# Seven-product gates in a two-layer encoder: a second tile for the raw weight sums, branch c run to its end first, wider gaps between the differences' transfers

## The chip, the cores and the metric

The kernel runs on one core of one Trainium2 chip. The metric is device time in microseconds (us) of one execution. Before the change it is 1827.98 us, the median of three runs (1826.03 to 1829.21).

## The reference

Two layers of an encoder over 512 positions with 1024 channels. In each layer three token mixers (differential attention, a convolution module, neighbourhood attention) give ya, yb and yc with 512 channels each. Each is projected to 1024 channels and multiplied by a sigmoid gate that is itself a projection of the normalised input.

```
h = rmsnorm(x, norm_mix[i])
proj = h @ w_in[i]
...
ga, gb, gc = jnp.split(jax.nn.sigmoid(gates), 3, axis=-1)
merged = (ga * (ya @ w_br_a[i]) + gb * (yb @ w_br_b[i])
          + gc * (yc @ w_br_c[i]))
x = x + merged @ w_o[i]
```

A SwiGLU feed-forward network and a gated embedding follow in each layer, and one norm at the end.

## The kernel before, in words

Channels lie on the 128 partitions and the 512 positions along the free axis, so a tensor of 1024 channels is eight tiles of 128x512. Everything is float32, and a matrix product runs as three matmuls for each block (`mm3`, L178): both operands are split into a high and a low part of a reduced float32 form, and high x high, high x low and low x high are summed. The high part is made by a copy on ScalarE (ACT, L144), the low part by a subtraction on VectorE (DVE, L158). So each weight is loaded by SyncE's DMA queue (SP), split by ACT and then by DVE, and used by TensorE (PE).

The order of the work in one layer, around the change: the gates of branch c (`gate_c`), the first two of branch b (`gate_b` m = 0, 1), the products of branch c (`branch_c`, one per m, with `w_br_c`), two more gates of branch b (m = 2, 3), then `merge_a`, then the convolution's norm, the rest of gate b, and the merge.

`merge_a` makes the gates of branch a by pairs of output tiles with a seven-product scheme (`gates`, L847): a 2x2 block product is done with seven products instead of eight. Its weights are a11, a12 and a22, as they are, and four sums of blocks, s1 to s4. The sums are built in a tile called the raw sums (`raw`, 128x1024). SP loads two blocks into it (L864, L865), GpSimd's queue (POOL) adds two more by accumulating DMAs (L869), ACT and DVE split the result into s1 and s2, then DVE turns the same tile in place into s3 and s4 (L161, L158), and these are split too. There is one such tile, named `gatec_v` in the profile, for all four pairs of a layer: the loads of a pair can start only when the splits of the pair before have read it. The other operands of the products are differences of the input (`t1` to `t4`), which `scaled` adds up on POOL into a DRAM buffer `tq` during an earlier stage (L265), and `differences` loads and splits by quarters during branch c.

PE does for each pair, in this order: a11 | s1, s3, a12 | s2, a22, s4. At the strokes (the `yield`s) `merge_a` puts in the products of a branch as a filling (`branch_pair`): for pair 0 those of branch c with m = 6 and 7, which `branch_c` leaves out, for the others those of branch a of the pair before. A holds s3's sum on top of a copy of C (a11's product), Q is a copy of A, and the copies are made by ACT (L144). The product with s4 is written into A as well, and must wait until ACT has copied A away. In the profile, PE's rows are `mergea_mm` for C, A and Q, `mergea_tr` or `branchc_tr` for T (the product of s1), `branchc_sc` for the filling of pair 0; `mergea_b` and `mergea_rp` are the splits of s4 and s3; `mergea_wh` and `mergea_wl` are the splits of weights and of s1 and s2.

A fourth strand is the aside chain (`aside`): 16 taps of the convolution for one block of channels. Each tap is an ACT instruction into one tile (`conv_rb`), which POOL then adds to the sum by an accumulating DMA (L593, `conv_z<-conv_rb`); the next tap can start only when that DMA has read the tile. Its steps are placed in ACT's queue behind certain instructions of the other stages (`beside`).

PE's order is that of the program. The queues of the other engines are ordered by the framework's scheduler by priority; weight loads and their splits are drawn ahead (`high_priority`). Every engine works through its queue in order, so an instruction that waits holds all behind it.

Of the kernel before, what the change touches and what calls it, by code (L numbers as in the profile page):

```python
# [15 lines left out]
ALU = mybir.AluOpType  # L16
# [4 lines left out]
P = 128  # L21
# [5 lines left out]
KD = 8  # L27
# [35 lines left out]
class Net:  # L63
# [181 lines left out]
    def scaled(self, xs):  # L245

        c = self.i * PAR_L
        self.nc.vector.tensor_scalar(self.neg[:, self.i * KD:self.i * KD + KD],
                                     self.parts[:, c:c + KD], -1.0, None, ALU.mult)
        for k, x in enumerate(xs):  # L250
            yield 1
            self.tt(x, x, self.rb, ALU.mult)
            self.hs.append(self.operand(x, self.par(self.i, "mix", k), "h"))
            f, n = self.sb("t", [P, 2, 256]), self.i * KD + k
            for half in range(2):
                g = self.par(self.i, "mix", k) if half == k % 2 else self.neg[:, n:n + 1]
                self.act(f[:, half], x[:, half * 256:half * 256 + 256], AF.Copy, scale=g)
            self.nc.gpsimd.dma_start(self.fd[:, k % 2 * 2:k % 2 * 2 + 2, k // 2], f)
        t1, t2, t3, t4 = (self.tq[:, n] for n in range(4))
        b11, b12, b21, b22 = (self.fd[:, n] for n in range(4))  # L260
        for out, src, add in ((t1, b11, 0), (t3, b22, 0), (t1, b12, 1), (t3, b12, 1), (t2, t1, 0),
                              (t2, b22, 1), (t4, t2, 0), (t4, b21, 1)):
            yield 4
            kw = dict(accum_op=ALU.add) if add else {}
            self.nc.gpsimd.dma_start(out, src, **kw)  # L265

# [186 lines left out]
    def layer(self, i, h, xsrc, xs):  # L453
        self.i, self.h = i, h
        zs, cs = [], []
        self.todo, self.other = self.taps(zs, cs), self.aside(zs)
        self.glu(zs)
        if i == 0:
            self.lambdas()
        yc, ya, yb = [], [], []  # L460
        sn, sd = {}, {}
        self.natten_in(0, sn, yc)
        self.drain(self.renorm)
        self.h = self.hs
        self.natten_v(sn)
        last = self.glu_last(zs)
        self.natten_in(1, sn, yc)
        next(last)
        self.natten_in(2, sn, yc)
        next(last)  # L470
        self.natten_in(3, sn, yc)
        acc, gb = [], []
        self.diff_in(0, sd, ya)
        self.diff_v(0, sd)
        self.diff_in(1, sd, ya)
        self.gate_c(acc, 0)
        self.diff_in(2, sd, ya)
        self.diff_v(1, sd)
        self.diff_in(3, sd, ya)
        for m in range(1, KD):  # L480
            self.gate_c(acc, m)
        self.bs, self.raw = [], self.sb("v", [P, 1024])
        for m in range(2):
            self.gate_b(gb, m, AF.Copy, None)
        for g in acc + gb:
            self.act(g, g, AF.Sigmoid, table="sigmoid")
        self.branch_c(acc, yc)
        for m in range(2, 4):
            self.gate_b(gb, m, AF.Sigmoid, "sigmoid")
        self.merge_a(yc, ya, acc)  # L490
        conv = self.run(self.conv(cs, yb))
        pairs = self.inputs()
        for m in range(4, KD):
            self.gate_b(gb, m, AF.Sigmoid, "sigmoid")
            for n in ((0, 1), (2,), (3,), ())[m - 4]:
                self.input_block(pairs, n)
        self.drain(conv)
        mg = self.merge_b(yb, acc, gb)
        ws = self.pair_weights(4)
        x, h = self.w_o(mg, xsrc)  # L500
        self.input_pair(ws, pairs, 4)
        h = self.ffn(h, x)
        return self.ple(h, x, xs, self.inputs())
# [305 lines left out]
    def branch_c(self, acc, ys):  # L809
        self.phase = "branchc"  # L810
        quarters = self.differences()
        for m in range(KD - 2):
            ps = self.ps("mm")
            self.gemm(ps, self.a["w_br_c"][self.i, m], ys)
            self.background(self.tt(acc[m], acc[m], ps, ALU.mult), self.bg["branchc"])
            next(quarters, None)
            if m % 3 == 2:
                next(quarters, None)
        for _ in quarters:
            pass  # L820

# [25 lines left out]
    def gates(self, m, out):  # L847

        self.phase = "mergea"
        nc, raw = self.nc, self.raw  # L850
        wg, wu = (self.a["w_ga"][self.i, m + u] for u in range(2))
        ws = {}
        lo, up = slice(0, 512), slice(512, 1024)

        def halve(hi, lo, src, names):
            self.split(hi, lo, src)
            for q, name in enumerate(names):
                c = slice(q * 512, q * 512 + 512)
                ws[name] = (hi[:, c], lo[:, c])

        wide = lambda: (self.sb("wh", [P, 1024], F32R), self.sb("wl", [P, 1024], F32R))
        with self.tc.high_priority(offset=min(self.w_ahead, self.tc.cur_priority - self.p0)):
            g, a22 = self.sb("wr", [P, 1024]), self.sb("r", [P, 512])
            nc.sync.dma_start(raw[:, lo], wg[:, lo])  # L864
            nc.sync.dma_start(raw[:, up], wu[:, up])  # L865
            nc.sync.dma_start(g, wg)
            nc.sync.dma_start(a22, wu[:, up])
            for q in (lo, up):
                nc.gpsimd.dma_start(raw[:, q], wu[:, lo], accum_op=ALU.add)  # L869
            halve(*wide(), g, ("a11", "a12"))  # L870
            halve(self.sb("kh", [P, 512], F32R), self.sb("a", [P, 512], F32R), a22, ("a22",))
            halve(*wide(), raw, ("s1", "s2"))
            self.stt(raw[:, lo], raw[:, lo], -1.0, a22, ALU.mult, ALU.subtract)
            self.tt(raw[:, up], g[:, up], raw[:, lo], ALU.subtract)
            for name, q, tag in (("s3", lo, "rp"), ("s4", up, "b")):
                halve(*(self.sb(tag, [P, 512], F32R) for _ in range(2)), raw[:, q], (name,))
        C, A, Q = (self.ps("mm", (P, 256)) for _ in range(3))

        def product(ps, w, b, first=False):
            wh, wl = ws[w]  # L880
            for k in range(4):
                c, both = slice(k * P, k * P + P), self.bs[k][b]
                self.mm3(ps, wh[:, c], wl[:, c], both[:, 0], both[:, 1], first and k == 0, k == 3,
                         skip_group_check=True)
                if k % 2:
                    self.chunk()

        gg, uu = self.sb("t", [P, 2, 256]), self.sb("t", [P, 2, 256])
        product(C, "a11", "b11", True)
        self.act(A, C, AF.Copy)  # L890
        yield
        T = self.ps("tr", (P, 256))
        product(T, "s1", "t3", True)
        self.act(uu[:, 0], T, AF.Copy)
        product(A, "s3", "t2")
        self.background(self.act(Q, A, AF.Copy), self.bg["mergea"])
        product(C, "a12", "b21")
        self.act(gg[:, 0], C, AF.Sigmoid, table="sigmoid")
        yield
        product(A, "s2", "t1")  # L900
        self.act(uu[:, 1], A, AF.Copy)
        product(Q, "a22", "t4")
        self.tt(uu[:, 1], uu[:, 1], uu[:, 0], ALU.add)
        last = self.tt(uu[:, 0], Q, uu[:, 0], ALU.add)
        product(A, "s4", "b22")
        self.act(gg[:, 1], A, AF.Sigmoid, table="sigmoid")
        self.beside(self.act(uu, uu, AF.Sigmoid, table="sigmoid", scale=-1.0))
        self.background(last, self.bg["mergea2"])
        out += [g.rearrange("p a b -> p (a b)") for g in (gg, uu)]
        yield  # L910
# [19 lines left out]
            take(acc[m + u], pb, m + u)  # L930
            yield

    def merge_a(self, yc, ys, acc):
        gs = []

        def times(a, pb, m):
            last = self.tt(a, a, pb, ALU.mult)
            self.background(last, self.bg["branchc"])

        def gated(a, pb, m):  # L940
            g = gs[m]
# [2 lines left out]

        for n in range(5):
            pair = self.gates(2 * n, gs) if n < 4 else iter(())
            if n:
                fill = self.branch_pair("w_br_a", ys, acc, 2 * n - 2, gated)
            else:
                fill = self.branch_pair("w_br_c", yc, acc, 6, times)  # L950
            for g in (pair, fill, fill, pair, fill, pair):
                next(g, None)

# [750 lines left out]
```

## Time and profile before

| | |
|---|---|
| median of three runs | 1827.98 us (1826.03 to 1829.21) |
| the profiled execution | 1828.74 us, of it the span 1827.0 us |
| mean granted TensorE clock | 0.983 |
| chain that ended last | PE 26% of the span, DVE 1%, all others 0% as the page rounds them |
| DMA | 289.02 MB, mean 158 GB/s |

Times in the rows are microseconds from the start of the span. A row of the timeline gives the start, the length, the engine, the line and the tiles (output first), and in brackets how long the engine had been idle before and whom it had waited for. The length of a PE row is that of one matmul from start to end; since they overlap, the time of a product is read from the starts. Layer 0's stage of the change lies at about 320 to 420 us, layer 1's at about 1224 to 1320 us.

### The profile page before, as it was taken

The numbers are of one execution on the slowest core, as the hardware profiler recorded it, in microseconds if no ns is written. First come the engines' busy times: TensorE is split into PE (matmuls) and PEld (weight loads), VectorE is DVE, ScalarE is ACT, GpSimd is POOL, SyncE is SP. The second block draws the span as 40 slices with busy tenths as digits, with TensorE's granted clock in tenths as the row PEclk, the third lists the DMA queues.
The fourth block names the chain that finished last, engine by engine and source line by source line (L and its number), as shares of the span: only waits on it lengthen the run. The fifth ranks groups of instructions, "written<-read, shape, count | busy, mean of one in ns | idle before, by whom it ended". The sixth has DMA issues, their size and how long they took to land. (4 is left out here: it accounts for less than half of the span.)

```text
span 1827.0 us, 26061 instructions
## 1 busy us (share of the span) xinstructions
PE 1769.6 (97%) x9258; PEld 1518.3 (83%) x9258; DVE 1427.7 (78%) x2366; ACT 1030.3 (56%) x1867; POOL 182.4 (10%) x208
## 2 busy tenths in 40 slices
PE   9999999887999999999999999998899999999998
PEld 7789888786888888888888888887778888888887
DVE  7877987756889778697787788787577996877876
ACT  5576556344577456474555655564445773655744
POOL 0100001121111011000010000011201210101000
PEclk9999999898999999999999999998899999999999
DMA  6885644574757556453459755356738573655432
GB/s 225 246 220 156 166 115 135 151 157 109 213 157 195 140 154 159 135 141 110 150 187 244 209 146 162 99 153 141 165 101 242 150 199 114 171 152 152 111 101 93
DMA packets 133954, 289.02 MB, mean 158 GB/s; under 512 B 18880, under 2 KB 29888, under 8 KB 133824
## 3 DMA queue, kind: packets, MB, share of 16 engines
q1 hardware_dynamic: 107920, 234.13, 41.7%
q0 software_dynamic: 25184, 51.92, 15.8%
q8 instruction: 73, 1.20, 0.3%
q10 hardware_dynamic: 720, 1.31, 0.2%
q14 instruction: 57, 0.47, 0.1%
HBM read 234.33 MB, written 19.92 MB: 139 GB/s over the span
## 5 line engine op out<-in xcount | busy, mean ns | idle before, releaser
L161 DVE SCALAR_TENSOR_TENSOR conv_z<-glu_z,pre_par,conv_z 128x512 f32<-128x512 f32 x210 | 157.0, 747 | 4.5 <-DMA conv_z<-conv_rb 1.6
L144 ACT ACTIVATE ffn_wh<-ffn_wr 128x1024 fp32r<-128x1024 f32 (+1 forms) x92 | 92.7, 1021 | 99.4 <-PE ffn_mm L181 66.4
L1160 POOL DMA_DIRECT2D ffn_qk<-w_fu x88 | 78.3, 972 | 589.6 <-DMA ffn_qk<-w_fu 277.9
L158 DVE TENSOR_TENSOR ffn_wl<-ffn_wr,ffn_wh 128x1024 fp32r<-128x1024 f32 (+1 forms) x92 | 107.1, 1175 | 21.0 <-ACT ffn_wh L144 20.5
L158 DVE TENSOR_TENSOR ffn_t<-ffn_mm,wo_rb 128x512 f32<-128x512 f32 (+1 forms) x46 | 31.1, 677 | 51.6 <-PE ffn_mm L182 51.6
L158 DVE TENSOR_TENSOR ffn_wl<-ffn_qk,ffn_wh 128x1024 fp32r<-128x1024 f32 x44 | 53.6, 1218 | 11.0 <-ACT ffn_wh L144 10.9
L144 ACT ACTIVATE ffn_wh<-ffn_qk 128x1024 fp32r<-128x1024 f32 x44 | 46.7, 1061 | 26.8 <-PE ffn_mm L181 16.2
L144 ACT ACTIVATE diff_a<-diff_sc,diff_s 128x512 f32<-128x512 f32 x32 | 22.1, 689 | 66.9 <-DVE diff_s L1074 66.6
L180 PE MATMUL ffn_mm<-ffn_v,ffn_wh 128*128 128x512 f32 x132 | 51.4, 389 | 0.0
L181 PE MATMUL ffn_mm<-ffn_v,ffn_wh 128*128 128x512 f32 x132 | 51.4, 389 | 0.0
L182 PE MATMUL ffn_mm<-ffn_v,ffn_wl 128*128 128x512 f32 x132 | 51.3, 389 | 0.0
L180 PE MATMUL ffn_mm<-ffn_y,ffn_wh 128*128 128x512 f32 x132 | 51.3, 389 | 0.0
L181 PE MATMUL ffn_mm<-ffn_y,ffn_wh 128*128 128x512 f32 x132 | 51.3, 389 | 0.0
L182 PE MATMUL ffn_mm<-ffn_y,ffn_wl 128*128 128x512 f32 x132 | 51.3, 389 | 0.0
L144 ACT ACTIVATE natten_wh<-natten_wr 128x1024 fp32r<-128x1024 f32 x24 | 25.3, 1056 | 40.4 <-PE natten_sc L734 21.5
L1194 PE MATMUL ffn_sc<-wo_h,ffn_wh 128*128 128x512 f32 x176 | 48.0, 394 | 0.0
L158 DVE TENSOR_TENSOR ffn_t<-ffn_t,ffn_e 128x256 f32<-128x256 f32 x84 | 46.2, 550 | 1.0 <-ACT ffn_e L144 0.9
L593 POOL DMA_DIRECT2D conv_z<-conv_rb x30 | 27.0, 899 | 180.5 <-ACT conv_rb L144 128.7
L1074 DVE TENSOR_REDUCE diff_s<-diff_sc 128x1 f32<-128x512 f32 x64 | 42.1, 682 | 2.2 <-PE diff_sc L981 2.2
L1194 PE MATMUL ffn_mm<-wo_h,ffn_wh 128*128 128x512 f32 x160 | 43.6, 394 | 0.0
L226 POOL TENSOR_TENSOR diff_rc<-diff_sm,pre_power 128x4 f32<-128x4 f32 x8 | 8.9, 1113 | 347.5 <-DVE diff_sm L161 347.5
L144 ACT ACTIVATE natten_b<-natten_b,natten_s 128x256 f32<-128x256 f32 x64 | 30.5, 500 | 21.1 <-DVE natten_s L767 21.0
(1038 smaller groups left out, 6393.5 us busy)
## 6 DMA issues: line engine op xcount, KB each, us to landing
ffn_qk<-w_fu POOLq DMA_DIRECT2D x88, 256.0 KB, 6.6
ffn_wr<-w_fg SPq DMA_DIRECT2D x44, 512.0 KB, 4.2
ffn_wr<-w_fd SPq DMA_DIRECT2D x32, 448.0 KB, 3.9
ffn_r<-w_fu SPq DMA_DIRECT2D x44, 256.0 KB, 2.8
ffn_qk<-w_fg SPq DMA_DIRECT2D x44, 256.0 KB, 3.3
ffn_qk<-w_fu SPq DMA_DIRECT2D x44, 256.0 KB, 3.5
natten_wr<-w_in SPq DMA_DIRECT2D x16, 512.0 KB, 5.3
diff_wr<-w_in SPq DMA_DIRECT2D x16, 512.0 KB, 4.5
```

The costliest lines, as they stand in the source:

```text
L144: i = self.nc.scalar.activation(out, in_, func, **kw)
L158: return self.nc.vector.tensor_tensor(out, a, b, op)
L161: return self.nc.vector.scalar_tensor_tensor(out, a, s, b, op0, op1)
L180: mm(out, wh, ah, start=first, stop=False, **kw)
L181: mm(out, wh, al, start=False, stop=False, **kw)
L182: mm(out, wl, ah, start=False, stop=last, **kw)
L226: nc.gpsimd.tensor_tensor(col, ms, self.power, ALU.pow)
L593: self.nc.gpsimd.dma_start(c, t, accum_op=ALU.add)
L1074: nc.vector.tensor_reduce(out=m[:, u:u + 1], in_=sc, op=ALU.max, axis=AX.X, negate=True)
L1160: nc.gpsimd.dma_start(q, wu[:, lo], accum_op=ALU.add)
L1194: mm(out, wh[:, c], bs[k][b], start=first and k == 0, stop=False, skip_group_check=True)
```

## The change

There are three edits.

1. In `scaled` eight units of other work instead of four stand between the transfers that add up `tq` (`yield 8`).
2. `branch_c` makes all eight products itself; the filling of pair 0 in `merge_a` is empty. The quarters of `differences` advance by one per product (before, by two after the third and the sixth).
3. A second tile holds raw sums (`gateb_y` in the names below); pairs 0 and 2 use the first, pairs 1 and 3 the second.

```diff
@@ scaled
-            yield 4
+            yield 8
             kw = dict(accum_op=ALU.add) if add else {}
             self.nc.gpsimd.dma_start(out, src, **kw)
@@ layer
-        self.bs, self.raw = [], self.sb("v", [P, 1024])
+        self.bs, self.raws = [], [self.sb("v", [P, 1024])]
...
-        self.merge_a(yc, ya, acc)
+        self.merge_a(ya, acc)
@@ branch_c
-        for m in range(KD - 2):
+        for m in range(KD):
...
             next(quarters, None)
-            if m % 3 == 2:
-                next(quarters, None)
@@ gates
-        nc, raw = self.nc, self.raw
+        nc, raw = self.nc, self.raws[m // 2 % 2]
@@ merge_a
-    def merge_a(self, yc, ys, acc):
+    def merge_a(self, ys, acc):
         gs = []
-
-        def times(a, pb, m):
-            last = self.tt(a, a, pb, ALU.mult)
-            self.background(last, self.bg["branchc"])
+        self.raws.append(self.sb("y", [P, 1024]))
...
-            if n:
-                fill = self.branch_pair("w_br_a", ys, acc, 2 * n - 2, gated)
-            else:
-                fill = self.branch_pair("w_br_c", yc, acc, 6, times)
+            fill = self.branch_pair("w_br_a", ys, acc, 2 * n - 2, gated) if n else iter(())
```

On TensorE, at pair 0 in layer 0: the end of a11 (mergea_mm) and what follows it, before the change.

```order
L180 MATMUL mergea_mm<-glu_h,mergea_wh 128x256
L181 MATMUL mergea_mm<-glu_h,mergea_wh 128x256
L182 MATMUL mergea_mm<-glu_h,mergea_wl 128x256
L180 MATMUL branchc_sc<-natten_y,branchc_wh 128x512
L181 MATMUL branchc_sc<-natten_y,branchc_wh 128x512
L182 MATMUL branchc_sc<-natten_y,branchc_wl 128x512
```

The same place after the change.

```order
L180 MATMUL mergea_mm<-glu_h,mergea_wh 128x256
L181 MATMUL mergea_mm<-glu_h,mergea_wh 128x256
L182 MATMUL mergea_mm<-glu_h,mergea_wl 128x256
L180 MATMUL mergea_tr<-branchc_qk,mergea_wh 128x256
L181 MATMUL mergea_tr<-branchc_qk,mergea_wh 128x256
L182 MATMUL mergea_tr<-branchc_qk,mergea_wl 128x256
```

Before, twelve matmuls of branch c stood between a11 and s1's product, and twelve more behind a12; now s1's product follows a11 at once, and those 24 stand ahead of gate b's m = 2.

On POOL's queue from the fourth norm of the heads (diff_rc) to the adds of the first gates (gatec_x), layer 0, before the change; gatec_v<-w_ga are the accumulations of raw sums, conv_z<-conv_rb those of the aside taps.

```order
L226 TENSOR_TENSOR diff_rc<-diff_sm,pre_power 128x4
L593 DMA conv_z<-conv_rb 128x512
L869 DMA gatec_v<-w_ga 128x512 x2
L593 DMA conv_z<-conv_rb 128x512
L869 DMA gatec_v<-w_ga 128x512 x2
L593 DMA conv_z<-conv_rb 128x512
L869 DMA gatec_v<-w_ga 128x512 x2
L943 DMA gatec_x<-mergea_t 128x512
L943 DMA gatec_x<-mergea_t 128x512
L869 DMA gatec_v<-w_ga 128x512
L593 DMA conv_z<-conv_rb 128x512
L869 DMA gatec_v<-w_ga 128x512
```

The same place after the change.

```order
L226 TENSOR_TENSOR diff_rc<-diff_sm,pre_power 128x4
L867 DMA gateb_y<-w_ga 128x512 x2
L593 DMA conv_z<-conv_rb 128x512
L867 DMA gatec_v<-w_ga 128x512 x2
L593 DMA conv_z<-conv_rb 128x512
L867 DMA gatec_v<-w_ga 128x512 x2
L867 DMA gateb_y<-w_ga 128x512
L593 DMA conv_z<-conv_rb 128x512
L938 DMA gatec_x<-mergea_t 128x512
L867 DMA gateb_y<-w_ga 128x512
L938 DMA gatec_x<-mergea_t 128x512
L593 DMA conv_z<-conv_rb 128x512
```

Pair 1's sums (gateb_y) now come first, pair 0's behind them and behind a tap; pair 2's (the second gatec_v) have moved ahead by one pair.

On SP's queue, from the loads of a11 and a12 (mergea_wr<-w_ga) on, before the change; mergea_wr<-w_br_a and branchc_wr are the weights of the fillings.

```order
L866 DMA mergea_wr<-w_ga 128x1024
L830 DMA branchc_t<-tq 128x2x256
L830 DMA branchc_t<-tq 128x2x256
L830 DMA branchc_t<-tq 128x2x256
L920 DMA branchc_wr<-w_br_c 128x512 x2
L866 DMA mergea_wr<-w_ga 128x1024
L864 DMA gatec_v<-w_ga 128x512
L865 DMA gatec_v<-w_ga 128x512
L920 DMA mergea_wr<-w_br_a 128x512 x2
```

The same place after the change.

```order
L864 DMA mergea_wr<-w_ga 128x1024
L864 DMA mergea_wr<-w_ga 128x1024
L862 DMA gateb_y<-w_ga 128x512
L863 DMA gateb_y<-w_ga 128x512
L918 DMA mergea_wr<-w_br_a 128x512 x2
L862 DMA gatec_v<-w_ga 128x512
L863 DMA gatec_v<-w_ga 128x512
L865 DMA mergea_r<-w_ga 128x512
L864 DMA mergea_wr<-w_ga 128x1024
```

The raw loads of pair 1 and the weights of branch a's first filling now stand ahead of the raw loads of pair 0. POOL's eight transfers into tq stand in the same order, with the same waits, before and after.

## The prediction

> **What bounds the kernel now.** The page's first rows come first: they say which engine is the bound.
>
> ```profile
> PE 1769.6 (97%) x9258; PEld 1518.3 (83%) x9258; DVE 1427.7 (78%) x2366; ACT 1030.3 (56%) x1867; POOL 182.4 (10%) x208
> ```
>
> TensorE (PE) works 97% of the span. A change that keeps its matmuls, as this one does, can win only PE's waits and what a lowered clock adds. So the next view is PE's waits, summed by instruction and releaser (us in total, times, longest).
>
> ```profile
> PE mergea_mm L180 <- ACT mergea_t L144: 26.5, 8, 5.4
> PE branchc_sc L180 <- ACT branchc_wh L144: 8.8, 2, 4.5
> PE conv_tr L629 <- ACT conv_rp L144: 8.8, 2, 4.4
> PE diff_tr L230 <- POOL diff_rc L226: 1.9, 2, 1.4
> ```
>
> The first two rows are in the stage that the change touches. Eight times, four pairs in two layers, the product with s4 waits for ACT's copy of A; twice the first product of the branch c fill waits for its weights. PE's timeline gives the places, with the idle time before each in brackets.
>
> ```profile
> 320.45 0.39 PE L180 MATMUL gateb_mm<-glu_h,gateb_wh 128*128 128x512 f32 x1
> 331.33 0.28 PE L180 MATMUL mergea_mm<-glu_h,mergea_wh 128*128 128x256 f32 x1
> 332.65 0.28 PE L182 MATMUL mergea_mm<-glu_h,mergea_wl 128*128 128x256 f32 x1
> 337.26 0.67 PE L180 MATMUL branchc_sc<-natten_y,branchc_wh 128*128 128x512 f32 x1 [4.33 <-ACT branchc_wh L144]
> 355.52 0.58 PE L180 MATMUL mergea_mm<-glu_h,mergea_b 128*128 128x256 f32 x1 [3.33 <-ACT mergea_t L144]
> 374.69 0.39 PE L180 MATMUL mergea_mm<-glu_h,mergea_b 128*128 128x256 f32 x1 [0.78 <-ACT mergea_t L144]
> 395.21 0.39 PE L180 MATMUL mergea_mm<-glu_h,mergea_b 128*128 128x256 f32 x1 [4.73 <-ACT mergea_t L144]
> 417.96 0.58 PE L180 MATMUL mergea_mm<-glu_h,mergea_b 128*128 128x256 f32 x1 [5.44 <-ACT mergea_t L144]
> ...
> 1240.64 0.80 PE L180 MATMUL branchc_sc<-natten_y,branchc_wh 128*128 128x512 f32 x1 [4.48 <-ACT branchc_wh L144]
> 1258.41 0.39 PE L180 MATMUL mergea_mm<-ple_h,mergea_b 128*128 128x256 f32 x1 [2.28 <-ACT mergea_t L144]
> 1276.80 0.39 PE L180 MATMUL mergea_mm<-ple_h,mergea_b 128*128 128x256 f32 x1 [1.08 <-ACT mergea_t L144]
> 1296.31 0.39 PE L180 MATMUL mergea_mm<-ple_h,mergea_b 128*128 128x256 f32 x1 [3.73 <-ACT mergea_t L144]
> 1318.75 0.58 PE L180 MATMUL mergea_mm<-ple_h,mergea_b 128*128 128x256 f32 x1 [5.13 <-ACT mergea_t L144]
> ```
>
> Between 320.45 and 331.33 stand the 48 matmuls of gate b's m=2, 3: 0.227 us a step. The twelve of a11 (331.33 to 332.65) step by 0.12. From one s4 product to the next PE has 84 steps of 0.12 and 24 of 0.227, 15.5 us; the spacings are 19.17, 20.52 and 22.75 in layer 0 and 18.39, 19.51 and 22.44 in layer 1. A stall costs more than itself, as three windows show (length, PE's busy time and matmuls, granted clock, DMA share, GB/s).
>
> ```profile
> 354.00:362.00 8.00, 6.48 (x29) 0.57 0.52 176
> 395.00:400.00 5.00, 4.79 (x26) 0.66 0.93 202
> 1276.00:1280.00 4.00, 3.21 (x26) 1.00 0.45 101
> ```
>
> After the stall of 3.33 the clock averages 0.57 over 8 us; after 1.08 it stays 1.00. Layer 0's 19.17 is 15.5 of work, 0.78 of stall and 2.9 of slow clock; layer 1's 18.39 holds 1.8 of it. On this the Trainium skill, "TensorE: Matmul & The Clock Gate", Part 1, speaks: the clock halves after about 3.4 us idle. By that, neither pair 0's 3.33 nor its 2.28 would slow it, the gain of 2.8 and 2.0 worked out below would fall away, and the time would be 1822.2. The trace says otherwise (0.57 after 3.33), and it decides.
>
> **Who holds the stalls.** ACT's and POOL's rows for the raw sums (gatec_v is their tile):
>
> ```profile
> 327.71 0.92 POOL L593 DMA_DIRECT2D conv_z<-conv_rb  x1 [10.56 <-DMA gatec_v<-w_ga]
> 328.37 2.06 POOL L869 DMA_DIRECT2D gatec_v<-w_ga  x2
> 335.20 1.06 ACT L144 ACTIVATE mergea_wh<-gatec_v 128x1024 fp32r<-128x1024 f32 x1 [2.46 <-DMA gatec_v<-w_ga]
> 353.19 1.06 ACT L144 ACTIVATE mergea_wh<-gatec_v 128x1024 fp32r<-128x1024 f32 x1 [3.81 <-DMA gatec_v<-w_ga]
> 377.71 0.63 ACT L144 ACTIVATE mergea_b<-gatec_v 128x512 fp32r<-128x512 f32 x1 [0.36 <-DVE gatec_v L158]
> 378.25 0.37 ACT L144 ACTIVATE mergea_mm<-mergea_mm 128x256 f32<-128x256 f32 x1
> ```
>
> At 335.20 ACT had waited for pair 0's sums, accumulated by POOL from 328.37; the weights of the fill stood behind them, so PE stood. At 353.19 it waited for pair 1's sums, which could be loaded only once pair 0 had let the one tile go, and pair 0's copy of A stood behind that. For pairs 2 and 3 the copy stands behind the serial chain of the aside taps (conv_rb on ACT, its accumulation on POOL, the next conv_rb):
>
> ```profile
> 380.86 0.70 ACT L144 ACTIVATE conv_rb<-glu_z,pre_par 128x512 f32<-128x512 f32 x1
> 389.25 0.72 ACT L144 ACTIVATE conv_rb<-glu_z,pre_par 128x512 f32<-128x512 f32 x1 [3.40 <-DMA conv_z<-conv_rb]
> 393.65 0.72 ACT L144 ACTIVATE conv_rb<-glu_z,pre_par 128x512 f32<-128x512 f32 x1 [1.06 <-DMA conv_z<-conv_rb]
> 401.89 0.72 ACT L144 ACTIVATE conv_rb<-glu_z,pre_par 128x512 f32<-128x512 f32 x1 [3.48 <-DMA conv_z<-conv_rb]
> 415.15 0.72 ACT L144 ACTIVATE conv_rb<-glu_z,pre_par 128x512 f32<-128x512 f32 x1 [2.48 <-DMA conv_z<-conv_rb]
> ...
> 1282.96 0.70 ACT L144 ACTIVATE conv_rb<-glu_z,pre_par 128x512 f32<-128x512 f32 x1
> 1290.31 0.72 ACT L144 ACTIVATE conv_rb<-glu_z,pre_par 128x512 f32<-128x512 f32 x1 [2.36 <-DMA conv_z<-conv_rb]
> 1315.94 0.72 ACT L144 ACTIVATE conv_rb<-glu_z,pre_par 128x512 f32<-128x512 f32 x1 [2.42 <-DMA conv_z<-conv_rb]
> ```
>
> The last three steps take 13.26 us, 4.4 each. Six steps from 380.86 would end at 407.3; they end at 415.15, 7.9 late: 4.0 in the first step (8.39) and 3.8 in the third (8.24). Layer 1 is 6.6 late, 2.95 in its first step. POOL shows the cause of the first:
>
> ```profile
> 382.94 0.87 POOL L869 DMA_DIRECT2D gatec_v<-w_ga  x1 [9.90 <-DMA gatec_v<-w_ga]
> 383.57 1.13 POOL L593 DMA_DIRECT2D conv_z<-conv_rb  x1
> ```
>
> The tap of 380.86 was accumulated only at 383.57, behind a sum of pair 2 that waited for its reload. The third step falls into the stretch whose DMA share is 0.93 (window 395 to 400).
>
> **The change, part by part**, against the profiled execution's 1828.74 us (0.76 above the median of the three runs).
>
> *Transfers further apart.* POOL's rows and their waits are the same in both kernels at this place, so it does nothing: 0.
>
> *Branch c to its end first.* 24 matmuls of 0.227, 5.45 us, stand before gate b instead of inside pair 0; that cancels. What goes is the fill that stood between a11 and s1. The stall of 4.33 doesn't go: s1 needs the sums themselves, behind which the fill's weights stood in ACT's queue. Count from gate b's m=2 (320.45 before). a11 ends at 12.4. The sums were usable at 14.75 (335.20); now SP and POOL take pair 1's before pair 0's. Lower bound: nothing lost, 14.75. Upper bound: 1 MB of SP loads (pair 1's sums, and w_br_a) and 0.5 MB of accumulations more ahead, nothing hidden, at the 202 GB/s of the window from 395: 7.4 us, 22. Which of the two it is nearer to, the DMA view of 318 to 356 shows (a digit and a rate for each 0.95 us, then an issue row: KB each, us to landing).
>
> ```profile
> DMA  9679899610029797979000298988820299930000
> GB/s 293 217 182 334 181 306 323 250 69 32 2 47 205 112 170 97 175 129 168 0 0 0 39 272 321 302 341 326 261 88 0 17 129 170 160 63 13 0 0 0
> ...
> gatec_v<-w_ga POOLq DMA_DIRECT2D x4, 256.0 KB, 5.5
> ```
>
> Between the raw loads (to 325) and the accumulations (from 328) some 3.5 us are nearly empty. At the 300 GB/s and more of the busiest slices the 1.5 MB are 5 us; 3.5 of them fit there. I take 14.75 + 1.3 = 16.0, the lower end being the nearer. Then s1 starts at 17.1, after ACT's 1.06, a stall of 4.7; its low halves cost 1 more (DVE's split follows ACT's); s3 waits about 1.3, since ACT's copy of T (0.37) and the split of s3 (0.63) now follow s1's end; slow clock 2.1. The stretch to pair 0's s4 was 355.52 − 320.45 − 5.45 = 29.6, of which work is 19.5 (48 steps of 0.227, 72 of 0.12) and stalls 7.7; the rest, 2.4, is slow clock and small waits. Now 19.5 + 4.7 + 1 + 1.3 + 2.1 + 0.2 = 28.8: **gain 0.8** a layer (from 2.1 at the lower bound to a loss of 5.2). Besides, DVE has a split of the differences ahead of the reduction that diff_tr waits for: **loss 0.3** (0 to 1.4, the longest of that row).
>
> *Second tile.* Pair 1's sums lie ready in the other tile, so pair 0's s4 stall (3.33; 2.28) shrinks to some 0.2, which is in the 28.8, and no slow clock follows. The spacing to pair 1's s4 becomes 15.5 + 0.7 (its own stall, since pair 2's sums now stand ahead of that copy) + 0.2 = 16.4: **gain 2.8 and 2.0**. Bounds: no gain, if pair 1's stall grows by as much; 3.6 and 2.9 with no stall at all.
>
> *The aside chain.* Pair 2's sums are reloaded one pair earlier, so POOL's conv_z no longer stands behind a waiting sum. The first step's 4.0 and 2.95 mostly go, the third's (DMA load) stays, since its loads remain: **gain 3.0 and 2.5**, from 0 to all of 7.9 and 6.6. The stalls at the s4 of pairs 2 and 3 (4.73 and 5.44; 3.73 and 5.13) can take it. conv_tr keeps its 4.4: both paths to it move along.
>
> Sum: layer 0, 0.8 + 2.8 + 3.0 − 0.3 = 6.3; layer 1, 0.8 + 2.0 + 2.5 − 0.3 = 5.0. Together 11.3: **1817.4 us**.
>
> The Trainium skill, "DMA: Bandwidth & Descriptors", "Issuing engines are not separate DMA queues", speaks against the change: transfers of SP and POOL share the same 16 engines, so pair 1's sums on both queues take bandwidth from pair 0's. No row of before shows both together; by this rule nothing hides, the landing is at the upper bound of 22, and the sum is 11.3 − 12.0, a loss of 0.7 (1829.4). The nearly empty slices speak against it.
>
> **The rivals.** (1) *The aside chain doesn't move*: its steps stay as slow, because conv_z now meets other accumulations on POOL. For it: POOL still has sums between the taps. Against: they no longer wait. Gain 3.3 + 2.5 = 5.8: 1822.9. (2) *Both delays go*, since the reloads leave the busy stretch too: 4.9 and 4.1 more, 1808.4. Against: ffn and gate weights are still loaded there. (3) *Slower: pair 0's sums come second.* On SP two loads of w_br_a stand ahead of them and wait for a weight slot of gate b; whatever stands there holds pair 0's loads, and PE has nothing left to do between a11 and s1. Each us counts fully, in both layers. It decides from 5.7 us a layer later than my 16.0, 21.7, just inside the upper bound of 22. At 24, the wait for the slot on top of that bound, it is 8.0 late, 16.0 in all: 1833.4. For it: the order on both queues. Against: the nearly empty 3.5 us. (4) *The change does not do what it says* for the transfers: certain, and in the sum at 0.
>
> **How the numbers follow.** Forecast (1813 to 1821) 0.42; rival 1 (1821 to 1824.3) 0.20; rival 2 (under 1813) 0.15; little or no gain, the landing between 19 and 23.5 (up to 1832.4), 0.14; rival 3 beyond that, 0.09. Rival 4 has no chance apart, being in each. What a measurement can tell from no change is 0.2%, 3.7 us. Faster 0.77, same 0.14, slower 0.09. The range for 8 in 10 runs from 1806 to 1827, leaving out the far ends of rivals 2 and 3.
>
> **What would show it.** Right: no s4 stall above 0.5 in pair 0, clock 1.00 through pair 1, a stall of 4 to 5 us before the first s1 product (mergea_tr), the first conv_rb step after pair 1 near 4.4. Wrong: a stall before s1 of 8 us or more (rival 3); conv_rb steps of 8 us twice as before (rival 1); stalls of pairs 2 and 3 under 1 us (rival 2); another spacing of the tq transfers on POOL.

## The result, and the profile after

The changed kernel takes 1812.24 us, the median of four runs (1809.84 to 1817.43), against 1827.42 for the kernel before on the same chip (four runs, 1826.03 to 1829.21). The ratio is 0.992, with a 95% interval of 0.9896 to 0.9945. The forecast was 1817.4 in a range of 1806 to 1827. The profiled execution took 1813.51 us, 15.2 less than the one of before.

First PE's waits after the change (us in total, times, longest):

```profile
PE mergea_tr L180 <- ACT mergea_wh L144: 10.3, 2, 5.7
PE conv_tr L629 <- ACT conv_rp L144: 9.9, 2, 5.6
PE mergea_mm L180 <- ACT mergea_t L144: 7.3, 4, 3.7
...
PE mergea_mm L180 <- ACT mergea_mm L144: 2.8, 2, 1.8
PE diff_tr L230 <- POOL diff_rc L226: 2.7, 2, 1.5
```

The row of the s4 products has gone from 26.5 us in eight waits to 7.3 in four. The wait for the filling's weights (8.8) is no longer there; in its place s1's product waits for pair 0's sums, 10.3. The row of 2.8 is new: pair 3's product with s2 waits for a copy on ACT (1.05 and 1.76). PE's timeline after the change gives the places, gate b's m = 2 first:

```profile
327.18 0.39 PE L180 MATMUL gateb_mm<-glu_h,gateb_wh 128*128 128x512 f32 x1
344.26 0.39 PE L180 MATMUL mergea_tr<-branchc_qk,mergea_wh 128*128 128x256 f32 x1 [4.60 <-ACT mergea_wh L144]
345.52 0.58 PE L182 MATMUL mergea_tr<-branchc_qk,mergea_wl 128*128 128x256 f32 x1 [0.76 <-DVE mergea_wl L158]
349.01 0.58 PE L180 MATMUL mergea_mm<-branchc_qk,mergea_rp 128*128 128x256 f32 x1 [0.99 <-ACT mergea_rp L144]
357.72 0.38 PE L180 MATMUL mergea_mm<-glu_h,mergea_b 128*128 128x256 f32 x1
373.34 0.38 PE L180 MATMUL mergea_mm<-glu_h,mergea_b 128*128 128x256 f32 x1
390.13 0.39 PE L180 MATMUL mergea_mm<-glu_h,mergea_b 128*128 128x256 f32 x1 [1.05 <-ACT mergea_t L144]
410.96 0.58 PE L180 MATMUL mergea_mm<-glu_h,mergea_b 128*128 128x256 f32 x1 [3.73 <-ACT mergea_t L144]
...
1239.23 0.58 PE L180 MATMUL mergea_tr<-branchc_qk,mergea_wh 128*128 128x256 f32 x1 [5.68 <-ACT mergea_wh L144]
1252.41 0.39 PE L180 MATMUL mergea_mm<-ple_h,mergea_b 128*128 128x256 f32 x1
1268.07 0.38 PE L180 MATMUL mergea_mm<-ple_h,mergea_b 128*128 128x256 f32 x1
1284.87 0.39 PE L180 MATMUL mergea_mm<-ple_h,mergea_b 128*128 128x256 f32 x1 [1.05 <-ACT mergea_t L144]
1305.69 0.39 PE L180 MATMUL mergea_mm<-ple_h,mergea_b 128*128 128x256 f32 x1 [1.51 <-ACT mergea_t L144]
```

The s4 products of pairs 0 and 1 don't wait at all, in either layer. The spacings of the four are now 15.62, 16.79 and 20.83 in layer 0 and 15.66, 16.80 and 20.82 in layer 1; the first is the 15.5 us of PE's work and nothing else. What stays is the wait before s1, and the s4 of pair 3. The clock behind the wait before s1 in layer 0 (windows of PE: length, busy time and matmuls, granted clock, DMA share, GB/s) is low until about 355, some 10 us:

```profile
344.00:348.00 4.00, 2.98 (x12) 0.59 0.00 0
348.00:352.00 4.00, 3.01 (x13) 0.50 0.62 194
352.00:356.00 4.00, 4.00 (x25) 0.63 0.38 134
```

The aside chain after the change, on ACT behind pair 1:

```profile
379.31 0.71 ACT L144 ACTIVATE conv_rb<-glu_z,pre_par 128x512 f32<-128x512 f32 x1
383.74 0.72 ACT L144 ACTIVATE conv_rb<-glu_z,pre_par 128x512 f32<-128x512 f32 x1 [1.31 <-DMA conv_z<-conv_rb]
388.14 0.72 ACT L144 ACTIVATE conv_rb<-glu_z,pre_par 128x512 f32<-128x512 f32 x1 [1.05 <-DMA conv_z<-conv_rb]
393.54 0.72 ACT L144 ACTIVATE conv_rb<-glu_z,pre_par 128x512 f32<-128x512 f32 x1 [2.94 <-DMA conv_z<-conv_rb]
...
408.15 0.72 ACT L144 ACTIVATE conv_rb<-glu_z,pre_par 128x512 f32<-128x512 f32 x1 [2.86 <-DMA conv_z<-conv_rb]
```

The first step is 4.43 (8.39 before), the third 5.40 (8.24). Six steps take 28.8 us instead of 34.3, and in layer 1 28.8 instead of 33.0.

**Where the time went.** By the two profiled executions, layer 0 and layer 1, gain positive:

| stretch | forecast | measured |
|---|---|---|
| wait at the last diff_tr | −0.3, −0.3 | −0.65, −0.13 |
| gate b m = 2 to pair 0's s4, without branch c's 5.45 | +0.8, +0.8 | −0.92, −2.06 |
| pair 0's s4 to pair 1's | +2.8, +2.0 | +3.55, +2.73 |
| pair 1's s4 to pair 3's | +3.0, +2.5 | +5.65, +4.33 |
| pair 3's s4 to conv_tr | 0, 0 | −0.18, +1.10 |
| conv_tr to gate b's next | 0, 0 | +1.34, +1.10 |
| sum | 11.3 | 15.9 |

The remaining −0.6 lies before the stage in layer 0.

### The profile page after: what moved, and what is told of

Same layout as the page of the kernel before. It is cut to its first block, busy times and chain, and to the rows that moved or that the text cites. A ratio compares the mean times of both kernels' runs of the same rounds, so it can differ in the third digit from the quotient of the medians.

```text
span 1811.7 us, 26084 instructions
## 1 busy us (share of the span) xinstructions
PE 1764.7 (97%) x9258; PEld 1514.6 (84%) x9258; DVE 1427.3 (79%) x2368; ACT 1030.4 (57%) x1869; POOL 181.9 (10%) x208
## 5 line engine op out<-in xcount | busy, mean ns | idle before, releaser
L158 DVE TENSOR_TENSOR diff_wl<-diff_wr,diff_wh 128x1024 fp32r<-128x1024 f32 x24 | 29.4, 1224 | 15.1 <-ACT diff_wh L144 15.1
```

Of the source, the lines that this page charges most:

```text
L158: return self.nc.vector.tensor_tensor(out, a, b, op)
```

## The experiments

The first edit needed no run: with `yield 4` put back into the changed kernel, the order of all instructions on all five queues is the same row for row. It does nothing. The ratios below are to the kernel before as it ran in the same series: 1827.50 us (median of fifteen runs) for the first four experiments, 1826.19 us (seven runs) for the last three.

**One part alone.** `move_only` has branch c first and one tile:

```diff
-        self.raws.append(self.sb("y", [P, 1024]))
...
-        nc, raw = self.nc, self.raws[m // 2 % 2]
+        nc, raw = self.nc, self.raws[0]
```

> Branch c to its end first, but one tile of raw sums as before. My theory (the second tile carries the gain, the move alone none): PE still waits 4 to 5 us for pair 0's sums, now before s1, and pair 0's s4 still waits 2 to 4 us because ACT holds its copy of A behind pair 1's sums; spacings of the s4 products about 19, 20.5 and 22.5 as before; the time 1827 to 1831. Rival (it was the fill's weights behind the sums that cost PE, so the move carries the gain): no stall over 1 us in pair 0, the time 1812 to 1820.

Measured: 1835.19 us (1832.98 to 1836.13), ratio 1.0047 (1.0033 to 1.0062), so slower than before, and by more than my theory said. PE's timeline of this kernel at pairs 0 and 1 of layer 0:

```profile
343.11 0.38 PE L180 MATMUL mergea_tr<-branchc_qk,mergea_wh 128*128 128x256 f32 x1 [4.04 <-ACT mergea_wh L144]
356.58 0.28 PE L180 MATMUL mergea_mm<-glu_h,mergea_b 128*128 128x256 f32 x1
361.33 0.50 PE L180 MATMUL mergea_sc<-diff_y,mergea_wh 128*128 128x512 f32 x1 [1.79 <-ACT mergea_wh L144]
379.38 0.58 PE L180 MATMUL mergea_mm<-glu_h,mergea_b 128*128 128x256 f32 x1 [4.12 <-ACT mergea_t L144]
```

The wait before s1 is there. I had expected pair 0's s4 to wait as before. It doesn't, because ACT's queue has the copies in another order; the wait has gone one step on, to the weights of branch a's filling (mergea_sc), which stand behind pair 1's sums, and to pair 1's s4, which before waited 0.78 and now 4.12. The spacings are 22.8, 20.3 and 23.1. The rival, that the move carries the gain, is out.

`tile_only` has two tiles and leaves branch c's last two products inside pair 0:

```diff
-        nc, raw = self.nc, self.raw
+        nc, raw = self.nc, self.raws[m // 2 % 2]
...
         gs = []
+        self.raws.append(self.sb("y", [P, 1024]))
```

> Second tile, but the two products of branch c with m = 6 and 7 left inside pair 0 as before. The second tile takes the place of operands that these products read, so it comes free only behind the second of them. My theory (the move is what lets the second tile be loaded early): pair 1's sums land about as late as before or later, pair 0's s4 keeps a stall of 3 us or more, the time 1824 to 1836. Rival (the tile carries the gain by itself): spacings of the s4 products 15.6, 16.8 and 20.8 as after, the time 1812 to 1817.

Measured: 1827.93 us (1824.31 to 1829.66), ratio 1.0003 (0.9993 to 1.0014): no change. PE's longest wait in the stage, and SP's and ACT's rows that explain it:

```profile
361.60 0.80 PE L180 MATMUL mergea_sc<-diff_y,mergea_wh 128*128 128x512 f32 x1 [7.11 <-ACT mergea_wh L144]
```

```profile
342.82 0.33 SPq L865 DMA_DIRECT2D gatec_v<-w_ga  x1
348.85 0.33 SPq L864 DMA_DIRECT2D gateb_y<-w_ga  x1
```

```profile
359.54 1.06 ACT L144 ACTIVATE mergea_wh<-gateb_y 128x1024 fp32r<-128x1024 f32 x1 [4.65 <-DMA gateb_y<-w_ga]
```

Pair 1's sums are loaded only at 348.85, when branch c's second product has let the place go, and behind pair 2's (342.82). ACT waits for them until 359.54, and PE 7.1 us at the weights behind them. The expected stall at pair 0's s4 isn't there (it stands at branch a's filling), but the time is as expected. From pair 1's s4 to pair 2's it takes 16.79 us (376.73 to 393.52), as the changed kernel does. The unchanged time hides a gain and a loss: from pair 1's s4 to pair 3's PE takes 38.89 and 37.66 us, some 4.3 less than before in each layer, and the first step of the aside chain behind pair 1 is down to 4.44 and 4.38; but from pair 0's s4 to pair 1's it takes 25.2 and 25.1, 6 and 7 more. So neither edit gains alone: one costs 0.5%, the other nothing, both together gain 0.8%. The move gives the second tile its place early enough, the tile takes the wait out of the pairs.

**The tap behind the sums.** `tap_first` is the kernel before, with one order changed on POOL; `tapped` collects the accumulations of the taps. PE's and SP's queues stay as they were. ACT's does not, and DVE's not quite: the scheduler also moved taps on ACT among the copies and splits of pairs 2 and 3 (the second tap behind pair 1 now stands ahead of a weight's split, at 382.83 and 383.46; before, behind it, at 389.25 and 384.78).

```diff
             for q in (lo, up):
-                nc.gpsimd.dma_start(raw[:, q], wu[:, lo], accum_op=ALU.add)
+                add = nc.gpsimd.dma_start(raw[:, q], wu[:, lo], accum_op=ALU.add)
+                if m == 6:
+                    self.behind(add, self.tapped[-7])
```

> The kernel before, with one edit: on POOL the accumulation of the tap behind pair 1 stands ahead of the accumulations of pair 3's sums instead of between them. My theory (that tap waited behind a sum whose tile was not free): the first step of the aside chain behind pair 1 shrinks from 8.4 and 7.4 us to about 4.4, the stalls at the s4 of pairs 2 and 3 shrink by about 3 us together in each layer, the time 1820 to 1824. Rival (the step is slow because of the DMA load, or the chain doesn't set those stalls): the time within 2 us of before.

Measured: 1820.62 us (1819.06 to 1823.01), ratio 0.9967 (0.9954 to 0.9979). Its chain on ACT, and POOL's rows:

```profile
378.18 0.71 ACT L144 ACTIVATE conv_rb<-glu_z,pre_par 128x512 f32<-128x512 f32 x1
382.83 0.72 ACT L144 ACTIVATE conv_rb<-glu_z,pre_par 128x512 f32<-128x512 f32 x1 [1.72 <-DMA conv_z<-conv_rb]
389.72 0.72 ACT L144 ACTIVATE conv_rb<-glu_z,pre_par 128x512 f32<-128x512 f32 x1 [1.47 <-DMA conv_z<-conv_rb]
```

```profile
379.30 0.86 POOL L594 DMA_DIRECT2D conv_z<-conv_rb  x1 [10.08 <-ACT conv_rb L144]
380.20 0.87 POOL L870 DMA_DIRECT2D gatec_v<-w_ga  x1
```

The first step is 4.65 instead of 8.39 in layer 0, and 5.91 instead of 7.35 in layer 1. From pair 1's s4 to pair 3's PE takes 39.36 instead of 43.27, and 40.34 instead of 41.95: 5.5 us in all, what the prediction had for this term. PE's gain there is the chain's: its six steps take 3.91 us less in layer 0 and 1.62 less in layer 1, and PE gains 3.91 and 1.61. By the medians this edit is worth 6.9 us, almost half of what the change brought; how much of it is POOL's order and how much the order on ACT that came with it was not taken apart.

**Pair 0's sums first.** `sums_first` is the changed kernel with the raw loads and accumulations of pair 0 issued behind branch c in the program, from a function of their own (`rawsums`, four lines of `gates`), at the priority of weights:

```diff
         self.branch_c(acc, yc)
+        with self.tc.high_priority(offset=min(self.w_ahead, self.tc.cur_priority - self.p0)):
+            self.rawsums(0)
```

> The changed kernel, with pair 0's raw loads and accumulations issued behind branch c's products in the program, so that on SP and POOL they stand ahead of the last weights of branch c and of pair 1's sums. My theory (after the change pair 0's sums are late only because SP holds them behind loads that wait for other slots; their own tile is free some 15 us earlier): the stalls before s1 (4.6 and 5.7 us, and 0.8 and 0.5 at its low half) go, with the slow clock behind them; 6 to 8 us less in each layer, the time 1796 to 1802. Rival (the landing is bound by the load on the DMA engines, or what now waits is branch c's weights and the differences): the time 1808 or more, with new PE waits before branch c or diff_tr.

Measured: 1796.62 us (1795.83 to 1797.23), ratio 0.9838 (0.9823 to 0.9852). SP's first raw load, then PE's rows:

```profile
287.73 0.38 SPq L851 DMA_DIRECT2D gatec_v<-w_ga  x1
```

```profile
319.19 0.32 PE L230 MATMUL diff_tr<-pre_ident,diff_rc 128*128 128x128 f32 x1 [2.03 <-POOL diff_rc L226]
329.48 0.39 PE L180 MATMUL gateb_mm<-glu_h,gateb_wh 128*128 128x512 f32 x1
341.79 0.28 PE L180 MATMUL mergea_tr<-branchc_qk,mergea_wh 128*128 128x256 f32 x1
349.35 0.38 PE L180 MATMUL mergea_mm<-glu_h,mergea_b 128*128 128x256 f32 x1
```

The tile is loaded at 288, some 42 us before gate b's m = 2 (329.48). In the changed kernel the same loads were issued at 329.72, behind these of SP:

```profile
327.38 0.33 SPq L862 DMA_DIRECT2D gateb_y<-w_ga  x1
328.88 0.80 SPq L918 DMA_DIRECT2D mergea_wr<-w_br_a  x2
329.72 0.43 SPq L862 DMA_DIRECT2D gatec_v<-w_ga  x1
```

The first of them waits for branch c's last matmul (326.96 to 327.35). I had expected the tile to be free some 15 us before its loads; it was 42. So pair 0's sums were late by their place in the queues: on SP behind these loads, on POOL behind pair 1's sums and a tap. The edit moves both places together, so it doesn't tell one from the other. With the sums early, PE has no wait over 0.3 us from gate b's m = 2 to pair 0's s4 in layer 0: 19.87 us, of which 19.5 are work. In layer 1 it takes 20.70, with one wait of 0.91. This version beats both kernels. It gives a little back at diff_tr (2.03 and 2.29, against 1.18 and 1.54 after the change).

**The same kernel again, and matmuls in the stall.** Side by side ran the changed kernel once more and `spare_products`, which puts 18 matmuls that nothing reads into the stall before s1:

```diff
+        if m == 0:
+            spare = self.ps("sc")
+            for n in range(6):
+                self.mm3(spare, *(w[:, :P] for w in ws["a11"]), *self.halves(self.h[n]), n == 0, n == 5)
         yield
         T = self.ps("tr", (P, 256))
```

> The changed kernel once more, for comparison on the same chip. Every theory expects 1810 to 1817, stalls before s1 of 4 to 6 us and the granted clock at 0.5 behind them.

> The changed kernel with 18 more matmuls of 128x512 on TensorE in each layer, between a11 and s1 of pair 0, into a tile that nothing reads: 4.1 us of work in a stall of 4.6 and 5.7. Nothing else moves. My theory (pair 0 came out worse than forecast because the clock stays low for about 5 us behind this stall, not 2): with PE busy the clock stays near 1.00, the stretch from s1 to pair 0's s4 falls from 13.5 us to 9 to 10, and the time falls by 6 to 9 us although work was added. Rival (the low clock has another cause, or the products of pair 0 wait for ACT and DVE anyway): the stretch and the time stay within 2 us, or the time rises.

Measured: the changed kernel 1813.04 (1811.70 to 1815.87), ratio 0.9929 (0.9913 to 0.9945); its profiled execution waits 6.63 and 6.22 before s1, more than the 4.60 and 5.68 of the first. With the 18 matmuls 1810.71 (1807.46 to 1814.08), ratio 0.9914 (0.9895 to 0.9934). The added work costs nothing, but the 6 to 9 us did not come: the intervals overlap. In layer 0 the clock does stay up (windows of PE, from 344):

```profile
344.00:348.00 4.00, 2.02 (x13) 1.00 0.00 0
348.00:352.00 4.00, 3.30 (x25) 1.00 0.78 250
352.00:356.00 4.00, 4.00 (x35) 1.00 0.42 109
```

and pair 0's products go from s1 to s4 in 10.55 us instead of 13.46 (12.50 in the second profile of the changed kernel). But PE then waits for the split of s3:

```profile
347.94 0.38 PE L180 MATMUL mergea_mm<-branchc_qk,mergea_rp 128*128 128x256 f32 x1 [0.94 <-ACT mergea_rp L144]
349.15 0.39 PE L182 MATMUL mergea_mm<-branchc_qk,mergea_rp 128*128 128x256 f32 x1 [0.70 <-DVE mergea_rp L158]
```

In layer 1 the clock fell to 0.50 all the same:

```profile
1241.00:1245.00 4.00, 3.59 (x15) 0.50 0.77 253
```

though no wait there was longer than 0.85, and the stretch took 12.34 instead of 13.18 (13.45 in the second profile). Counted from gate b's m = 2, pair 0's s4 comes 3.7 and 2.4 us earlier than in that second profile, but the two profiled executions differ by only 1.9 us: some of this is lost again elsewhere, which was not followed up. So with the stall filled the clock stayed up in layer 0 and not in layer 1, and part of what the low clock costs is hidden behind ACT and DVE. Of my theory the cause fits layer 0 alone; the price of 6 to 9 us does not hold.

**The reduction first.** `reduce_first` is `sums_first` with the differences' second quarter one product later:

```diff
-            next(quarters, None)
+            if m != 1:
+                next(quarters, None)
```

> As sums_first, with the second quarter of the differences taken up one product later, so that on DVE the reduction that diff_tr waits for stands ahead of the split that waits for the transfer of tq. My theory: the stall at diff_tr (2.0 and 2.3 us in sums_first) shrinks to 0.5 to 1.5, no clock is lost behind it, the time is 2 to 5 us below sums_first, 1792 to 1795. Rival (the quarters come late for s1 then, or the norm's own chain sets the stall): the time as sums_first, 1796 to 1798, or above.

Measured: 1795.73 (1794.20 to 1796.59), ratio 0.9829 (0.9813 to 0.9846): as `sums_first` within what the intervals tell. I had expected 1792 to 1795. The stall at diff_tr did shrink (2.03 to 0.65, 2.29 to 0.88), and another came (PE's row, then ACT's):

```profile
342.23 0.38 PE L180 MATMUL mergea_mm<-branchc_qk,mergea_rp 128*128 128x256 f32 x1 [2.11 <-ACT mergea_mm L144]
```

```profile
337.97 0.63 ACT L144 ACTIVATE mergea_rp<-gatec_v 128x512 fp32r<-128x512 f32 x1 [4.19 <-DVE gatec_v L161]
```

ACT waits for DVE's s3, behind which its copy of C stands; DVE has the later splits of the differences ahead of it. The mechanism of the diff_tr wait was right, and its gain went to a new wait, at s3 and not, as the rival had it, at s1.

## Why the prediction held, and where it was off

**Right.** The transfers of `tq` did nothing. Pair 0's s4 stall went, no slow clock followed, and the spacing to pair 1's came to 15.6 in both layers; the 16.4 forecast allowed 0.7 for a wait behind pair 2's sums, which didn't come. The fill's wait did not go but moved to s1: in layer 0 the sums were usable at 343.15, which is 15.97 behind gate b's m = 2, forecast 16.0, and s1 started at 17.08, forecast 17.1. So close an agreement is luck: in layer 1 the sums were usable at 17.05, and in the second profile of the changed kernel at 18.00 and 17.59. The upper bound of 22, at which no transfer hides, was not reached. That PE would lose there was in the sum, and `sums_first` shows why: the place of these transfers in their queues. Rival 3 named the right place, though not the size that would make the change slower.

**Luck in the sum.** Pair 0 came out 4.6 us worse than forecast in the two layers together, and the other rows 9.1 better; the total is off by 4.6 because they partly cancel. The median, 1812.24, lies just below 1813, in the band that the prediction gave to rival 2 with a chance of 0.15; 1813.04 for the second set of runs lies just above, in the forecast's own. The sign of rival 2, stalls of pairs 2 and 3 under 1 us, did not show: they are 1.05 and 3.73, and 1.05 and 1.51.

**Off, pair 0.** The gain of 0.8 was a loss of 0.9 and 2.1. The step that failed is the term of the slow clock, 2.1 us. In layer 0 s1 to s4 took 13.46 us; the products are 7.2 of it (60 steps of 0.12) and the waits 1.75, so 4.5 went to the clock; over both profiles of the changed kernel and that of `move_only` it is 3.9 to 4.8. I had taken the price from the stall inside the filling, whose matmuls are longer (0.227 us a step, 1.8 and 2.4 us lost in the two layers before), and not asked what the clock would do to the products behind. In layer 1 the landing was later too (s1 at 18.15). `spare_products` tried to measure the price apart and got 2.3 us in all, within its spread: how much of it could be won without the stall itself is open.

**Off, the aside chain.** The mechanism was right and 3.0 and 2.5 were too little for what pairs 2 and 3 gained, 5.65 and 4.33. Here too PE's gain is nearly the chain's: its six steps take 5.45 us less in layer 0 and 4.15 less in layer 1. That `tap_first` gains 5.5, exactly the term, is again partly luck: by layers it is 3.9 and 1.6 against 3.0 and 2.5, and other steps moved with the first (in layer 0 the second grew from 4.40 to 6.89, the third fell from 8.24 to 4.64). What the forecast left out is that in the changed kernel the third step also shrinks, from 8.24 to 5.40, and from 7.95 to 5.30 in layer 1. That is part of what rival 2 foretold, but not for its reason: the reloads of pair 3's sums were over before the third step already before the change (378.25 and 379.51). I had said that the loads in that step would hit the chain as before. In the changed kernel gate b's next weights were loaded at 391.10, 3.0 us behind the start of that tap (388.14), where before they came 1.1 us behind it (394.79 and 393.65), so that the tap's accumulation now has a start on them. All nine profiles bear this out in both layers: in the four places where these weights are loaded 0.8 to 1.1 us behind the tap (the kernel before and `move_only`) the third step takes 7.95 to 8.24 us, and in the fourteen where it is 2.95 or 2.96 it takes 4.63 to 5.42, in `tap_first` too, which has only one tile. No edit moved these loads alone, so that this is the cause is strongly suggested and not isolated. One reading in the prediction was also wrong: the sums that held the tap at 382.94 were pair 3's, not pair 2's. Pair 2's were long accumulated (365.81). The mechanism is the same, one pair on. On POOL a sum of pair 3 still stands ahead of a tap after the change, but one tap earlier: it is the tap behind pair 0, whose successor starts only at 379.31, so nothing waits for it:

```profile
365.98 0.87 POOL L867 DMA_DIRECT2D gateb_y<-w_ga  x1 [9.53 <-DVE conv_z L161]
366.63 1.12 POOL L593 DMA_DIRECT2D conv_z<-conv_rb  x1
```

**Off, conv_tr.** The 1.3 and 1.1 us behind it were not in the sum. The waits ahead of it are about as long or longer (4.28 and 5.65, before 4.40 twice); the clock came back sooner (in layer 0 it was 0.50 from 437 to 443 before; after the change 0.51 from 430 to 433 and 0.92 from 433 to 436). In layer 0, conv_tr and gate b's next product after the change, and the latter before it:

```profile
430.32 0.79 PE L629 MATMUL conv_tr<-conv_rp,pre_onesr 128*128 128x512 f32 x1 [4.28 <-ACT conv_rp L144]
...
435.27 0.40 PE L180 MATMUL gateb_mm<-glu_h,gateb_wh 128*128 128x512 f32 x1
```

```profile
443.43 0.40 PE L180 MATMUL gateb_mm<-glu_h,gateb_wh 128*128 128x512 f32 x1
```

That is 4.95 us instead of 6.29 (437.14 to 443.43). In the second profile of the changed kernel it is 6.07, and 5.86 in layer 1, and over all nine profiles it lies between 4.95 and 6.44. So most of it is no gain of the change but the spread of the clock from run to run.

## What to carry to other kernels

A second buffer is worth what its place in the queues allows: ask when the place it takes comes free, and what its transfers are put ahead of. Two edits that each do nothing, or harm, can gain together, so a part tried alone doesn't settle it. And where an engine waits for a transfer, look first at how long the target had been free: here pair 0's tile had been free for some 40 us, and issuing its transfers earlier won about as much again as the whole change.

## What the runs showed of the hardware

The granted clock did not follow the length of a stall by one rule. Behind the stall of 4.60 in layer 0 of the changed kernel it was low for some 10 us, in which PE waited 0.76 and 0.99 more; behind the stall of 4.28 at conv_tr for about 3 (and for about 6 in another run of the same kernel). In layer 1 of `spare_products` it fell to 0.50 behind waits of 0.85 and 0.76, while in layer 0 of the same run it stayed at 1.00 behind 0.77 and 0.76. An estimate of what a stall costs beyond itself was off by a factor of two here (2.1 us forecast, 4.5 measured).
